# Best entries' rows and conditioning sums behind the linear attention's last step, in a fused decoder block on one Trainium2 core

## The chip, the cores and the metric

The kernel runs on one core of a Trainium2 chip. A core has a matrix engine (TensorE, PE in the profile), a vector engine (VectorE, DVE), an activation engine (ScalarE, ACT), a general engine (GpSimd, POOL) and a queue engine that issues transfers (SyncE, SP). Each engine runs its instructions in the order in which they were written to it and waits at an instruction whose inputs or buffers aren't ready. The metric is the device time of one execution in microseconds (us).

## The reference

One layer of a decoder block for 1024 tokens of width 1024. Two branches work on the same normalized input: a gated linear attention in chunks of 64 tokens, and a chunked gated MLP. Their gated outputs are added, projected by `w_out`, and added to the input. Then an expert mixer with product keys adds, for each token and each of 8 heads, the 16 best of 16384 rank-one experts. The norm ahead of each part has a scale and a shift that a dense layer (`w_ada`) makes from the conditioning vector `c`.

```
q, k, v, g, al, sgu, sgv, gate_a, gate_s = split(modulate(rms_norm(x), shift, scale) @ w_in)
state = diag(a_t) state + k_t^T v_t;  o_t = q_t state          # 4 heads, dk 128, dv 256
x = x + gate * ((norm(o) * silu(g), gated MLP) @ w_out)
h2 = modulate(rms_norm(x), shift2, scale2)
s = keys(h2 @ w_q);  entries, weights = top-16 of (top-16 x top-16)
x = x + gate2 * sum over heads and entries: weight * gelu(h2 . down[e]) * up[e]
```

(`modulate(h, shift, scale)` is h (1 + scale) + shift.)

## The kernel before, in words

The tokens are worked on in two halves of 512, each four blocks of 128. For a half, the columns of the input projection are streamed in groups of 512: V0, V1, QK0, the attention's heads 0 and 1, QK1, heads 2 and 3, and then the gates and the MLP; after them come `w_out` and `w_q`. A group is eight steps (`stream`, L1262), one for each 128 rows of its weights. In a step a weight tile `wt` arrives through SP's queue (L1248), ScalarE rounds it to `wh` (L1251), DVE takes the rest `wl = wt - wh` (L1252), and TensorE runs three products for each of four accumulators (L181 to L189). There are four `wt`, four `wh` and `wl`, and four accumulator banks.

After every step `step()` gives turns to queues of side work, which are Python generators that issue a few instructions and yield. Those that matter here:

- The **conditioning sums** (`ada_row`, L1139, with `ada_acc`, L1099): rows of `w_ada`, 128x1024 at a time (`wada`, L1103, on SP's queue, like the stream's weights), are multiplied by a column of `c` and added up on DVE, the first by L1106 and the other seven by L1108. This is done in the first half. The finished rows are joined by L1150 and L1154.
- The **routing** of the half before: `rare` (L391 to L447) handles the few tokens whose entries need another look; it gathers their scores from DRAM (L428, on POOL) and takes their maxima (L204 and on).
- The **direct rows** (`direct_rows`, L739): the best entry of every token and head of the first half, 4 blocks x 8 heads = 32 "entries", worked on during the second half. For each, POOL gathers a row of the down table and a row of the up table for each of 128 tokens (L752); DVE takes the dot product with `h2` (L764), ScalarE the GELU (L766), DVE the weight (L767, one column), and DVE adds the weighted up-row to the block's sum (L773; the first head of a block goes to L769 or a multiply).

The wide rows (`wada`, `adacc`, `uvd`, and the attention's outputs `ot`, which hold four) share one pool of eight 128x1024 tiles.

The attention's head (`gla_head`, L1402) transposes the keys (L1406), makes the in-chunk products (L1411, L1412), masks them by one DVE instruction, the *copy* into `at` (L1414), and goes through four token blocks: a state product (L1420), the output from `at` and from the state (L1422, L1423), and the *state update* on DVE (L1424). Ahead of it the queries leave their accumulators through L1378 to L1380 and the keys through L1395 to L1398. Side work gets its turns here too: `qdir.pump(RD)` (L1417), four times a head.

A pump has a rate: at 0.62 it advances its queue 62 times in 100 calls. `RD` is that rate for the direct rows in the stream's steps and in the heads. What a program order gives is then only a proposal: a scheduler goes over the instructions of all engines with its own model of their durations and fixes the order on each engine. `tc.issue_after(ins)` adds to an instruction the rule that it stands behind `ins` on its engine; `hlast`, `zlast` are earlier uses of it.

## Time and profile before

| | us |
|---|---|
| median of 3 runs | 1461.24 (1458.94 to 1463.65) |
| profiled execution, whole | 1465.81 |
| its span, first to last instruction | 1464.1 |
| TensorE busy | 1360.1 |
| VectorE busy | 1093.3 |
| ScalarE busy | 736.0 |
| GpSimd busy | 292.2 |
| mean granted TensorE clock | 0.967 |

A row such as `L764 DVE ... uvd<-uvd,h2d` is an instruction or a group of them: line of the kernel, engine, operation, and the tiles written and read. Brackets hold the idle time of the engine just ahead and what ended it. TensorE's matmuls take less time at a higher granted clock; a clock of 0.5 means half of full speed.

### The profile page before, as it was taken

The numbers are of one execution on the slowest core, as the hardware profiler recorded it, in microseconds if no ns is written. First come the engines' busy times: TensorE is split into PE (matmuls) and PEld (weight loads), VectorE is DVE, ScalarE is ACT, GpSimd is POOL, SyncE is SP. The second block draws the span as 40 slices with busy tenths as digits, with TensorE's granted clock in tenths as the row PEclk, the third lists the DMA queues.
The fourth block names the chain that finished last, engine by engine and source line by source line (L and its number), as shares of the span: only waits on it lengthen the run. The fifth ranks groups of instructions, "written<-read, shape, count | busy, mean of one in ns | idle before, by whom it ended". The sixth has DMA issues, their size and how long they took to land.

```text
span 1464.1 us, 19632 instructions
## 1 busy us (share of the span) xinstructions
PE 1360.1 (93%) x6004; PEld 1041.2 (71%) x6004; DVE 1093.3 (75%) x3114; ACT 736.0 (50%) x1611; POOL 292.2 (20%) x275
## 2 busy tenths in 40 slices
PE   3999999999998999998989999999988999888996
PEld 2778867888876887776777777887767876444553
DVE  6684768433467688988779888778889877888775
ACT  4464333333345545474434677566655555555542
POOL 0000001000000022432352133221111123543331
PEclk7999999999998999998999999999998999999998
DMA  9652544323349554767587689896687678998984
GB/s 323 218 188 96 195 150 147 108 94 102 131 152 318 175 202 147 257 203 255 195 293 261 220 308 348 294 351 217 225 330 260 213 246 315 345 357 312 404 305 167
DMA packets 120836, 345.00 MB, mean 236 GB/s; under 512 B 15033, under 2 KB 24505, under 8 KB 108690
## 3 DMA queue, kind: packets, MB, share of 16 engines
q0 software_dynamic: 32064, 165.95, 31.2%
q1 hardware_dynamic: 70992, 133.20, 27.2%
q10 hardware_dynamic: 17666, 44.53, 8.5%
q8 instruction: 48, 0.79, 0.2%
q14 instruction: 66, 0.54, 0.1%
HBM read 319.40 MB, written 24.23 MB: 235 GB/s over the span
## 4 chain that ended last, share of the span: by engine, by line
PE 58%; DMA 13%; DVE 12%; issue 9%; ACT 4%; POOL 2%; ACTq 0%; SPq 0%; DVEq 0%; POOLq 0%
PE mm L181 10%; PE mm L182 10%; PE mm L184 10%; PE acc L606 6%; PE mm L187 4%; PE mm L188 4%; PE mm L189 4%; DMA wada<-in_w_ada_dram 3%; DMA uvd<-in_down_dram,dix 2%; DMA uv<-in_tab_dram,ix 2%; DVE wl L1252 2%; POOL uvd L752 1%; DVE uv L580 1%; PE aux L1645 1%; PE hps L578 1%
## 5 line engine op out<-in xcount | busy, mean ns | idle before, releaser
L1251 ACT ACTIVATE wh<-wt 128x512 fp32r<-128x512 f32 x368 | 228.4, 628 | 311.1 <-PE mm L182 123.5
L1252 DVE TENSOR_TENSOR wl<-wt,wh 128x512 fp32r<-128x512 f32 x368 | 248.3, 685 | 145.6 <-ACT wh L1251 73.4
L181 PE MATMUL mm<-wh,hTh 128*128 128x512 f32 x672 | 266.1, 398 | 2.4 <-ACT wh L1251 2.3
L182 PE MATMUL mm<-wh,hTl 128*128 128x512 f32 x672 | 262.9, 393 | 0.0
L184 PE MATMUL mm<-wl,hTh 128*128 128x512 f32 x672 | 211.1, 396 | 0.0
L181 PEld LDWEIGHTS mm<-wh,hTh 128*128 128x128 f32 x672 | 127.2, 189 | 35.9 <-ACT wh L1251 5.9
L182 PEld LDWEIGHTS mm<-wh,hTl 128*128 128x128 f32 x672 | 127.0, 189 | 26.2
L184 PEld LDWEIGHTS mm<-wl,hTh 128*128 128x128 f32 x672 | 125.6, 189 | 27.8 <-issue 1.5
L525 POOL DMA_INDIRECT uv<-in_tab_dram,ix x74 | 79.7, 1077 | 250.3 <-ACT ix L557 176.0
L187 PE MATMUL mm<-wh,hTh 128*128 128x512 f32 x224 | 91.7, 418 | 10.1 <-ACT hTh L1209 5.5
L182 PE MATMUL mm<-hTl,wh 128*128 128x512 f32 x240 | 96.0, 400 | 0.0
L181 PE MATMUL mm<-hTh,wh 128*128 128x512 f32 x240 | 95.4, 397 | 0.0
L188 PE MATMUL mm<-wl,hTh 128*128 128x512 f32 x224 | 90.0, 402 | 0.8 <-DVE wl L1252 0.8
L189 PE MATMUL mm<-wh,hTl 128*128 128x512 f32 x224 | 88.3, 396 | 0.0
L580 DVE SCALAR_TENSOR_TENSOR uv<-uv,hps 128x512 f32<-128x512 f32 x112 | 75.0, 681 | 17.7 <-DMA uv<-in_tab_dram,ix 9.8
L187 PE MATMUL mm<-hTh,wh 128*128 128x256 f32 (+1 forms) x208 | 71.9, 350 | 7.6 <-DVE q L1379 6.8
L188 PE MATMUL mm<-hTl,wh 128*128 128x256 f32 (+1 forms) x208 | 70.9, 342 | 3.2 <-DVE hTl L173 3.2
L184 PE MATMUL mm<-hTh,wl 128*128 128x512 f32 x240 | 70.7, 396 | 0.3 <-DVE wl L1252 0.3
L752 POOL DMA_INDIRECT uvd<-in_down_dram,dix x32 | 36.9, 1154 | 168.0 <-DVE ts L359 44.7
L189 PE MATMUL mm<-hTh,wl 128*128 128x256 f32 (+1 forms) x208 | 69.7, 340 | 0.7 <-DVE wl L1252 0.7
L618 DVE SCALAR_TENSOR_TENSOR vl<-uv,r,vh 128x512 fp32r<-128x512 f32 x84 | 61.6, 746 | 10.0 <-ACT vh L617 7.3
L606 PE MATMUL acc<-uv,W 128*128 128x512 f32 x128 | 62.7, 613 | 5.6 <-ACT W L595 4.3
(933 smaller groups left out, 2896.2 us busy)
## 6 DMA issues: line engine op xcount, KB each, us to landing
wt<-in_w_inp_dram SPq DMA_DIRECT2D x224, 256.0 KB
wt<-in_w_qp_dram SPq DMA_DIRECT2D x80, 256.0 KB
wada<-in_w_ada_dram SPq DMA_DIRECT2D x32, 512.0 KB
wt<-in_w_outp_dram SPq DMA_DIRECT2D x64, 256.0 KB
wada<-in_w_ada_dram SPq DMA_DIRECT2D x32, 256.0 KB
s_d<-so ACTq DMA_DIRECT2D x28, 256.0 KB
xr<-in_x_dram ACTq DMA_DIRECT2D x8, 512.0 KB
x_d<-x ACTq DMA_DIRECT2D x8, 512.0 KB
```

What stands on the lines that cost most here:

```text
L181: nc.tensor.matmul(ps, lh, rh, start=False, stop=False)
L182: nc.tensor.matmul(ps, *((lh, rl) if feat else (ll, rh)), start=False, stop=False)
L184: nc.tensor.matmul(ps, *((ll, rh) if feat else (lh, rl)), start=False, stop=False)
L187: nc.tensor.matmul(ps, lh, rh, start=first, stop=False)
L188: nc.tensor.matmul(ps, lh, rl, start=False, stop=False)
L189: return nc.tensor.matmul(ps, ll, rh, start=False, stop=last).ins
L525: nc.gpsimd.indirect_dma_start(out=dst[:], out_offset=None, in_=src, in_offset=off)
L580: nc.vector.scalar_tensor_tensor(uv[0][:, sl], uv[0][:, sl], 1.0, hps, op0=OP.mult, op1=OP.mult, accum_out=r[:, 2 + n:3 + n])
L606: ins = nc.tensor.matmul(acc[:, sl], W, v[:, sl], start=first, stop=last).ins
L618: nc.vector.scalar_tensor_tensor(vl, v, r[:, 5:6], vh.bitcast(F32), op0=OP.mult, op1=OP.subtract)
L1251: nc.scalar.activation(wh, wt, AF.Identity)
L1252: nc.vector.tensor_tensor(wl, wt, wh.bitcast(F32), op=OP.subtract)
```

## The change

Four edits. (1) A list `crit` holds the last issued DVE instruction of the attention's chain: the last query or key operation (L1380, L1398), the copy (L1414) or a state update (L1424). The dot products and adds of the direct rows and the conditioning sums from the second on are issued behind it on DVE (`behind_crit`). (2) The direct rows' rate in the heads is 0.75 in place of 0.62, and in the stream's steps it is 1 in the first five of a group's eight steps and 0 in the last three. (3) `ada_acc` issues the load of the weights' row of step k+1 ahead of its sum of step k, with a yield between. (4) `rare` yields three times in place of once after the gather of its scores.

```diff
--- before.py
+++ after.py
@@ -45,7 +45,7 @@
 EB = 2
 WS = 4
 WT = 4
-RD = 0.62
+RD = 0.75
 UVC = 4
 RING = (1, 0, 1, 0, 2, 0)
 RING9 = (2, 0, 1, 2, 0, 2, 1, 0, 2)
@@ -428,7 +428,8 @@
         nc.gpsimd.indirect_dma_start(out=sc.rearrange("p c k -> p (c k)"), out_offset=None,
                                      in_=s_g[gi].rearrange("b p (h k) -> (b p h) k", h=PH),
                                      in_offset=bass.IndirectOffsetOnAxis(ap=ix, axis=0))
-        yield
+        for _ in range(3):
+            yield
         tv = r2.tile([P, 1, 2, TOPK], F32, name="qtv")
         ti = r2.tile([P, 1, 2, TOPK], U32, name="qti")
         for c in range(2):
@@ -734,7 +735,10 @@
         while b not in done:
             qr.pump()
 
-    zlast = []
+    zlast, crit = [], []
+
+    def behind_crit():
+        return tc.issue_after(crit[0]) if crit else nullcontext()
 
     def direct_rows(t4, bs):
         todo = [(b, h) for b in bs for h in range(PH)]
@@ -761,7 +765,8 @@
                 y = rowp.tile([P, D], F32, name="yd", tag="row")
             u, v = ents.pop(k)
             r = r2.tile([P, 2], F32, name="rdr", bufs=4)
-            nc.vector.scalar_tensor_tensor(u, u, 1.0, h2s[b], op0=OP.mult, op1=OP.mult, accum_out=r[:, 0:1])
+            with behind_crit():
+                nc.vector.scalar_tensor_tensor(u, u, 1.0, h2s[b], op0=OP.mult, op1=OP.mult, accum_out=r[:, 0:1])
             with tc.issue_after(zlast[0]):
                 nc.scalar.activation(r[:, 1:2], r[:, 0:1], AF.Gelu)
             nc.vector.tensor_tensor(r[:, 1:2], r[:, 1:2], dcol(dgtq, b, h), op=OP.mult)
@@ -770,7 +775,8 @@
             elif h == 0:
                 nc.vector.tensor_scalar(y, v, r[:, 1:2], None, op0=OP.mult)
             else:
-                nc.vector.scalar_tensor_tensor(y, v, r[:, 1:2], y, op0=OP.mult, op1=OP.add)
+                with behind_crit():
+                    nc.vector.scalar_tensor_tensor(y, v, r[:, 1:2], y, op0=OP.mult, op1=OP.add)
             if h == PH - 1:
                 nc.scalar.dma_start(y_d[b], y)
                 summed.add(b)
@@ -1098,15 +1104,25 @@
 
         def ada_acc(c):
             acc = t4("adacc")
-            for k in range(KD):
+            wts = []
+
+            def fetch(k):
                 wt = t4("wada")
                 nc.sync.dma_start(wt, w_ada[k * P:(k + 1) * P, c * D:(c + 1) * D])
+                wts.append(wt)
+
+            fetch(0)
+            for k in range(KD):
+                if k + 1 < KD:
+                    fetch(k + 1)
+                yield acc
+                wt = wts.pop(0)
                 if k == 0:
                     with tc.issue_after(hlast[1]):
                         nc.vector.tensor_scalar(acc, wt, sc[:, 0:1], None, op0=OP.mult)
                 else:
-                    nc.vector.scalar_tensor_tensor(acc, wt, sc[:, k:k + 1], acc, op0=OP.mult, op1=OP.add)
-                yield acc
+                    with behind_crit():
+                        nc.vector.scalar_tensor_tensor(acc, wt, sc[:, k:k + 1], acc, op0=OP.mult, op1=OP.add)
 
         def ada_cols(kp):
             accs = []
@@ -1267,6 +1283,7 @@
                     weights_ahead(len(srcs) if pre else LOOK + 1)
                     ws = [made.pop(0) for _ in srcs]
                     body(k, ws, pss)
+                    rate["d"] = 1.0 if k < 5 else 0.0
                     step()
                 for i in range(npsum):
                     evac(i, pss[i])
@@ -1377,7 +1394,7 @@
                         q4 = v4c(qs)
                         nc.vector.scalar_tensor_tensor(q4[:, :, 0], p4[:, :, 0], DK ** -0.5, e4[:, :, 0], op0=OP.mult, op1=OP.mult)
                         nc.vector.scalar_tensor_tensor(q1, p4[:, :, 1], DK ** -0.5, e4[:, :, 1], op0=OP.mult, op1=OP.mult)
-                        nc.vector.tensor_tensor(q4[:, :, 1], q1, last(0), op=OP.mult)
+                        crit[:] = [nc.vector.tensor_tensor(q4[:, :, 1], q1, last(0), op=OP.mult).ins]
                         qk[h] = [qs, q1]
                     else:
                         kk = gl.tile([P, 4, 3, 64], F32, name="kk")
@@ -1395,7 +1412,7 @@
                         nc.vector.tensor_tensor(kk[:, :, 0:3:2], p4, v4c(eGi), op=OP.mult)
                         nc.vector.tensor_tensor(kk[:, :, 1], p4[:, :, 0], d4[:, :, 0], op=OP.mult)
                         nc.vector.tensor_tensor(k4[:, :, 1], p4[:, :, 1], d4[:, :, 1], op=OP.mult)
-                        nc.vector.tensor_tensor(k4[:, :, 0], kk[:, :, 1], last(1), op=OP.mult)
+                        crit[:] = [nc.vector.tensor_tensor(k4[:, :, 0], kk[:, :, 1], last(1), op=OP.mult).ins]
                         qk[h] += [kk, kt]
                 return f
 
@@ -1411,7 +1428,7 @@
                     nc.tensor.matmul(aps_[:, p, 0:64], kk[:, p, 0:2], qs[:, p * P:p * P + 64], start=True, stop=True)
                     nc.tensor.matmul(aps_[:, p, 64:P], kk[:, p, 1:3], q1[:, p], start=True, stop=True)
                 a = at[h % 2]
-                nc.vector.copy_predicated(a, amask.unsqueeze(1).to_broadcast([P, 4, P]), aps_)
+                crit[:] = [nc.vector.copy_predicated(a, amask.unsqueeze(1).to_broadcast([P, 4, P]), aps_).ins]
                 hc = slice(h * DV, (h + 1) * DV)
                 for p in range(4):
                     qdir.pump(RD)
@@ -1421,7 +1438,8 @@
                     ops = gauxt([P, DV])
                     nc.tensor.matmul(ops, a[:, p], vt[p][:, hc], start=True, stop=False)
                     nc.tensor.matmul(ops, qs[:, p * P:(p + 1) * P], s_in, start=False, stop=True)
-                    nc.vector.scalar_tensor_tensor(s_out, s_in, eglt[h][:, p, 2:3], sps, op0=OP.mult, op1=OP.add)
+                    crit[:] = [nc.vector.scalar_tensor_tensor(s_out, s_in, eglt[h][:, p, 2:3], sps,
+                                                              op0=OP.mult, op1=OP.add).ins]
                     nc.scalar.activation(ot[p][:, hc], ops, AF.Identity)
                     jk = gl.tile([P, DV], F32, name="jk", bufs=1)
                     nc.scalar.activation(jk, ot[p][:, hc], AF.Square, accum_out=sso[:, p, h:h + 1])
```

The scheduler turns these into the following orders. The lines of the changed file are a few higher: L769 is what was L764 (dot), L772 was L767, L779 was L773 (add), L1122 was L1106 and L1125 was L1108 (conditioning sum), L1166 and L1170 were L1150 and L1154, L1268 was L1252 (`wl`), L1314 was L1297, L1431 was L1414 (copy), L1441 was L1424 (state update).

VectorE in the first half, from head 2's copy (into `at_309`) on, before:

```order
L1414 COPY_PREDICATED at_309<-amask,gaux 128x512
L1424 SCALAR_TENSOR_TENSOR S_1_304<-S_0_303,egl_894,aux 128x256
L1108 SCALAR_TENSOR_TENSOR adacc<-wada,sc,adacc 128x1024
L1252 TENSOR_TENSOR wl<-wt,wh 128x512 x2
L1108 SCALAR_TENSOR_TENSOR adacc<-wada,sc,adacc 128x1024
L1252 TENSOR_TENSOR wl<-wt,wh 128x512
L1108 SCALAR_TENSOR_TENSOR adacc<-wada,sc,adacc 128x1024
L1424 SCALAR_TENSOR_TENSOR S_0_303<-S_1_304,egl_894,aux 128x256
L1108 SCALAR_TENSOR_TENSOR adacc<-wada,sc,adacc 128x1024
```

and in the changed kernel:

```order
L1431 COPY_PREDICATED at_309<-amask,gaux 128x512
L1125 SCALAR_TENSOR_TENSOR adacc<-wada,sc,adacc 128x1024 x2
L1268 TENSOR_TENSOR wl<-wt,wh 128x512 x4
L1166 TENSOR_TENSOR adarow<-adarow,aux 1x512 x2
L1170 SCALAR_TENSOR_TENSOR adarow<-adarow,nrow 1x1024
L1268 TENSOR_TENSOR wl<-wt,wh 128x512
L1122 TENSOR_SCALAR adacc<-wada,sc 128x1024
L1441 SCALAR_TENSOR_TENSOR S_1_304<-S_0_303,egl_893,aux 128x256
L1441 SCALAR_TENSOR_TENSOR S_0_303<-S_1_304,egl_893,aux 128x256
```

Head 2's first state update (`S_1_304`) stood right behind the copy; now two conditioning sums, four `wl`, the joining of rows, another `wl` and the first product of the next sum stand between.

VectorE a little later, up to head 3's copy (into `at_311`) and its first state updates, before:

```order
L1108 SCALAR_TENSOR_TENSOR adacc<-wada,sc,adacc 128x1024 x2
L1424 SCALAR_TENSOR_TENSOR S_0_303<-S_1_304,egl_894,aux 128x256
L1108 SCALAR_TENSOR_TENSOR adacc<-wada,sc,adacc 128x1024
L1252 TENSOR_TENSOR wl<-wt,wh 128x512
L1106 TENSOR_SCALAR adacc<-wada,sc 128x1024
L1252 TENSOR_TENSOR wl<-wt,wh 128x512
L1108 SCALAR_TENSOR_TENSOR adacc<-wada,sc,adacc 128x1024
L1414 COPY_PREDICATED at_311<-amask,gaux 128x512
L1424 SCALAR_TENSOR_TENSOR S_1_307<-S_0_306,egl_899,aux 128x256
L1252 TENSOR_TENSOR wl<-wt,wh 128x512
L1424 SCALAR_TENSOR_TENSOR S_0_306<-S_1_307,egl_899,aux 128x256
```

and in the changed kernel:

```order
L1441 SCALAR_TENSOR_TENSOR S_1_304<-S_0_303,egl_893,aux 128x256
L1441 SCALAR_TENSOR_TENSOR S_0_303<-S_1_304,egl_893,aux 128x256
L1268 TENSOR_TENSOR wl<-wt,wh 128x512 x2
L1441 SCALAR_TENSOR_TENSOR S_1_304<-S_0_303,egl_893,aux 128x256
L1441 SCALAR_TENSOR_TENSOR S_0_303<-S_1_304,egl_893,aux 128x256
L1268 TENSOR_TENSOR wl<-wt,wh 128x512
L1431 COPY_PREDICATED at_311<-amask,gaux 128x512
L1441 SCALAR_TENSOR_TENSOR S_1_307<-S_0_306,egl_898,aux 128x256
L1441 SCALAR_TENSOR_TENSOR S_0_306<-S_1_307,egl_898,aux 128x256
L1314 BN_STATS bst<-svg 128x6 x2
L1441 SCALAR_TENSOR_TENSOR S_1_307<-S_0_306,egl_898,aux 128x256
```

The conditioning sums that stood among head 2's state updates and ahead of head 3's copy are gone from there; the next three stand behind head 3's updates.

VectorE in the second half, from head 2's last state update (`S_0_303`) to head 3's first two, before:

```order
L1424 SCALAR_TENSOR_TENSOR S_0_303<-S_1_304,egl_5839,aux 128x256
L1252 TENSOR_TENSOR wl<-wt,wh 128x512
L764 SCALAR_TENSOR_TENSOR uvd,rdr<-uvd,h2d 128x1024
L1252 TENSOR_TENSOR wl<-wt,wh 128x512
L767 TENSOR_TENSOR rdr<-rdr,dgt_0_140 128x1
L773 SCALAR_TENSOR_TENSOR yd<-uvd,rdr,yd 128x1024
L764 SCALAR_TENSOR_TENSOR uvd,rdr<-uvd,h2d 128x1024
L1414 COPY_PREDICATED at_311<-amask,gaux 128x512
L767 TENSOR_TENSOR rdr<-rdr,dgt_1_141 128x1
L1424 SCALAR_TENSOR_TENSOR S_1_307<-S_0_306,egl_5844,aux 128x256
```

and in the changed kernel:

```order
L1441 SCALAR_TENSOR_TENSOR S_0_303<-S_1_304,egl_5828,aux 128x256
L769 SCALAR_TENSOR_TENSOR uvd,rdr<-uvd,h2d 128x1024
L1268 TENSOR_TENSOR wl<-wt,wh 128x512
L772 TENSOR_TENSOR rdr<-rdr,dgt_0_140 128x1
L769 SCALAR_TENSOR_TENSOR uvd,rdr<-uvd,h2d 128x1024
L772 TENSOR_TENSOR rdr<-rdr,dgt_0_140 128x1
L1431 COPY_PREDICATED at_311<-amask,gaux 128x512
L779 SCALAR_TENSOR_TENSOR yd<-uvd,rdr,yd 128x1024
L1441 SCALAR_TENSOR_TENSOR S_1_307<-S_0_306,egl_5833,aux 128x256
```

The add that stood ahead of head 3's copy stands behind it now, ahead of head 3's first state update, and the copy follows on a dot whose entry is one earlier: 26 dots and 21 adds come before the copy in place of 27 and 22. Further ahead, two dots and an add that stood before head 0's state updates stand between them. From L204 of `rare` in the second half to the query evictions (L1378 before) the rows of both orders are the same, and so is the place of L428 in GpSimd's order. The loads of `wada` on SP's queue are spread among more loads of `wt`.

## The prediction

> **What bounds the kernel now.** I read the first parts of the page, then TensorE's waits, then the timeline at the three longest waits in the stretch that the change touches, then the granted clock around them.
>
> ```profile
> span 1464.1 us, 19632 instructions
> PE 1360.1 (93%) x6004; PEld 1041.2 (71%) x6004; DVE 1093.3 (75%) x3114; ACT 736.0 (50%) x1611; POOL 292.2 (20%) x275
> PE 58%; DMA 13%; DVE 12%; issue 9%; ACT 4%; POOL 2%; ACTq 0%; SPq 0%; DVEq 0%; POOLq 0%
> ```
>
> TensorE is busy for 1360.1 of 1464.1 us, so at most 104 us are idle in all, and a change of order on VectorE (DVE) can win only what TensorE waits for plus what its clock loses after a wait. The chain gives DVE 12% and DMA 13%. TensorE's waits say which instructions those are (columns: total us, times, longest):
>
> ```profile
> PE mm L187 <- DVE q L1379: 6.8, 1, 6.8
> PE gaux L1422 <- DVE rdr L767: 4.2, 1, 4.2
> PE gaux L1422 <- DVE at L1414: 3.4, 1, 3.4
> ```
>
> Call the 3.4 wait A (first half), the 6.8 wait B and the 4.2 wait C (both second half). A in the timeline (start, duration, engine, line; in brackets the idle time before and what ended it):
>
> ```profile
> 187.60 0.75 DVE L1106 TENSOR_SCALAR adacc<-wada,sc 128x1024 f32<-128x1024 f32 x1 [2.22 <-DMA wada<-in_w_ada_dram]
> 190.26 0.39 PE L188 MATMUL mm<-wl,hTh 128*128 128x512 f32 x1
> 190.49 0.40 PE L189 MATMUL mm<-wh,hTl 128*128 128x512 f32 x1
> 192.32 1.28 DVE L1108 SCALAR_TENSOR_TENSOR adacc<-wada,sc,adacc 128x1024 f32<-128x1024 f32 x1 [3.37 <-DMA wada<-in_w_ada_dram]
> 193.52 0.72 DVE L1414 COPY_PREDICATED at<-amask,gaux 128x512 f32<-128x512 int32 x1
> 194.29 0.70 PE L1422 MATMUL gaux<-vt,at 128*128 128x256 f32 x2 [3.40 <-DVE at L1414]
> ```
>
> Head 3's masked copy (L1414), which TensorE needs, stands behind a conditioning sum (L1108), and that sum waited 3.37 us for its weights' row. C is the same picture with a gathered row of the best entries:
>
> ```profile
> 748.87 1.28 DVE L773 SCALAR_TENSOR_TENSOR yd<-uvd,rdr,yd 128x1024 f32<-128x1024 f32 x1 [3.79 <-DMA uvd<-in_up_dram,dix]
> 750.21 1.23 DVE L764 SCALAR_TENSOR_TENSOR uvd<-uvd,h2d 128x1024 f32<-128x1024 f32 x1
> 751.36 0.72 DVE L1414 COPY_PREDICATED at<-amask,gaux 128x512 f32<-128x512 int32 x1
> 752.14 1.22 PE L1422 MATMUL gaux<-vt,at 128*128 128x256 f32 x2 [4.17 <-DVE rdr L767]
> ```
>
> The page names L767 there; it is an operation on one column behind the copy, and the copy at 751.36 is what was missing. B is different:
>
> ```profile
> 662.02 0.49 DVE L204 MAX8 qtv<-qsc 128x8 f32<-128x128 f32 x2 [3.10 <-DMA qsc<-s_d,qix]
> 664.20 0.39 PE L189 MATMUL mm<-hTh,wl 128*128 128x512 f32 x1
> 670.51 0.42 DVE L1378 SCALAR_TENSOR_TENSOR qs<-mm,eG 128x256 f32<-128x256 f32 x1
> 671.40 0.77 PE L187 MATMUL mm<-hTh,wh 128*128 128x512 f32 x1 [6.82 <-DVE q L1379]
> ```
>
> DVE loses 3.10 us on the rare tokens' score gather and works off its backlog until 670.51; only then do the query evictions free TensorE's banks. What a wait costs beyond itself is in the windows (us, busy, granted clock, DMA share, GB/s):
>
> ```profile
> 186.00:190.90 4.90, 4.89 (x30) 1.00 0.46 134
> 194.30:199.00 4.70, 4.70 (x14) 0.64 0.54 167
> 664.60:671.40 6.80, 0.00 (x0) 0.65 0.96 360
> 671.40:676.70 5.30, 5.29 (x13) 0.50 0.73 259
> 752.10:756.00 3.90, 3.86 (x11) 0.57 0.93 337
> 800.00:1250.00 450.00, 428.58 (x1982) 0.98 0.77 276
> ```
>
> Behind A 4.70 us ran at 0.64, which loses 4.70 x 0.36 = 1.7; behind B 5.30 x 0.50 = 2.65; behind C 3.90 x 0.43 = 1.7. So A is worth 5.1, B 9.5, C 5.9, at most 20.5 us together.
>
> [...]
>
> **The change part by part.** The durations of what is moved:
>
> ```profile
> L764 DVE SCALAR_TENSOR_TENSOR uvd<-uvd,h2d x32: 1204/1218/1240, 519.2 to 773.2; 128x1024 f32<-128x1024 f32 x32
> L773 DVE SCALAR_TENSOR_TENSOR yd<-uvd,rdr,yd x28: 1256/1278/1285, 526.2 to 785.8; 128x1024 f32<-128x1024 f32 x28
> L1108 DVE SCALAR_TENSOR_TENSOR adacc<-wada,sc,adacc x28: 1264/1284/1289, 68.5 to 226.6; 128x1024 f32<-128x1024 f32 x28
> L1150 DVE TENSOR_TENSOR adarow<-adarow,aux x8: 667/668/676, 101.7 to 240.9; 1x512 f32<-1x512 f32 x8
> ```
>
> No operation is added or removed: 32 dots, 28 adds and 28 conditioning sums run as before, and the DMAs are the same in number and size. All of the effect is order.
>
> *Wait A, conditioning sums behind the critical step, rows fetched one ahead.* In the new order head 3's copy stands behind one `wl` and head 2's state updates, and no conditioning sum stands between head 2's first state update and head 3's last one; the next three sums come after it. TensorE also has the eight split matmuls that it had between the products of L1411 and L1422 ahead of the transposes now, so the copy is asked for about 2 us earlier, measured from the end of L1411: a matmul every 0.23 us (190.26 to 190.49), eight of them 1.8 us. The copy itself takes 0.72, of which two `aux` matmul pairs cover some, so I leave 0.5 us of idle time. Gain: 3.40 - 0.5 + 1.7 = 4.6.
> The other side is head 2. Between its copy and its first state update now stand two sums (2 x 1.28), four `wl` (4 x 0.69), two row adds (2 x 0.67), one 1.21-us row operation, another `wl` and the first product of the next sum (0.75): 9.3 us. TensorE's second state product (L1423) was moved behind some 46 more matmuls, about 46 x 0.23 = 10.6 us, so it is covered if those sums don't wait. They can wait:
>
> ```profile
> DVE adacc L1108 <- DMA wada<-in_w_ada_dram: 13.7, 13, 3.4
> SPq L1103 <- DMA wada<-in_w_ada_dram: 24.3, 11, 3.4
> ```
>
> The wait is 1.05 us on average (13.7/13), and fetching a step ahead takes most of an average wait away; the longest, 3.4, would pass the cover of 1.3 by 2.1. Against the fetch stands SP's own queue: the rows' loads wait there for a free buffer (24.3 us in 11 waits, so 2.2 each), the stream's weights wait behind them, and each step ahead holds one buffer more out of the eight. I take -0.6 for head 2 and -0.5 for the weights; the bounds are 0 and -2.1 - 2.2 = -4.3. Net of A: +3.5, between +0.3 and +5.1.
>
> *Wait C, direct rows.* In the new order 26 dots and 21 adds stand ahead of head 3's copy, where 27 and 22 stood. What the copy waits for last is then the 26th dot, which began at 743.14 before, and not the 22nd add at 748.87. But the pace of these rows is set by gathers, as the first of these rows shows, and the gather of the next entry goes out when a dot or add has freed its buffer:
>
> ```profile
> DVE uvd L764 <- DMA uvd<-in_down_dram,dix: 16.0, 9, 5.2
> DVE yd L773 <- DMA uvd<-in_up_dram,dix: 4.9, 2, 3.8
> 719.15 1.22 DVE L764 SCALAR_TENSOR_TENSOR uvd<-uvd,h2d 128x1024 f32<-128x1024 f32 x1 [2.92 <-DMA uvd<-in_down_dram,dix]
> 743.14 1.23 DVE L764 SCALAR_TENSOR_TENSOR uvd<-uvd,h2d 128x1024 f32<-128x1024 f32 x1 [0.48 <-DMA uvd<-in_down_dram,dix]
> ```
>
> From 719.15 to 743.14 five entries pass, 4.8 us each. In the new order two dots and an add that stood ahead of head 0's state updates now stand between them, so the chain of gathers runs up to 0.75 of an entry late, 3.6 us: the 26th dot begins between 743.1 and 746.8, the copy between 744.4 and 748.0, and TensorE, which stopped at 748.0, waits 0 to 0.7 for it. The 22nd add now stands between the copy and head 3's first state update. With its gather at 748.87 to 752.5 it ends at 750.1 to 753.8, the update straight behind it, and TensorE can use about 1.7 us of other work meanwhile (to 749.7): a wait of 0.9 to 4.6 in place of 4.17. Best, 3.3 + 1.7 = +5.0; worst, -0.4 - 0 = -0.4, and with a further add behind it, -3.8 - 1.7 = -5.5. I take the middle of the first two, +2.5 with its share of the clock.
>
> *Rows in five of eight steps, 0.75 in the heads.* Before, 32 steps gave 32 x 0.62 = 19.8 entries and the heads' 16 pumps 9.9, 29.7 in all; the rest was drained after head 3. Now 4 x 5 = 20 and 16 x 0.75 = 12, exactly 32. The drain of two entries (2 x 2.5 us of DVE) goes away, and it was hidden: TensorE has no wait on L764 or L773 in its list. Worth 0. The two dots and the add among the state updates of head 0 are 2 x 1.22 + 1.28 = 3.7 us of DVE where TensorE has split matmuls to run; bounds 0 and -3.7, taken -1.0.
>
> *Three yields after the rare gather.* The place of that gather in POOL's order and of MAX8 (L204) in DVE's order, with all rows from there to L1378, are the same in both orders. So B stays: 0, and 9.5 if it went after all.
>
> *What follows.* Behind the heads the order of the later groups, of the routing and of the first entries is reshuffled on all engines. Between 800 and 1250 TensorE is idle for 450 - 428.6 = 21.4 us, in waits of which nearly all are short; a reshuffle can win or lose some fifth of that. Taken 0, with 4 to either side.
>
> **Sum.** +3.5 + 2.5 - 1.0 + 0 = 5.0 us. The profiled execution took 1465.81 (span 1464.1 and 1.7 around it), so it would take 1460.8; it lies 4.6 above the median of the runs, 1461.24, and on that scale the forecast is **1456.2 us**.
>
> **The rivals.** *Only A is won:* C's wait moves to the state update behind the 22nd add, whole. Then 3.5 - 1.0 - 0.4 = +2.1, so 1459. For it speaks the 3.79-us wait on that very gather; against it, that one entry less stands ahead of the copy.
> *B goes too:* the rare score chain is pulled away from the query evictions, 1456.2 - 9.5 = 1446.7. For it: three steps are worth 3 x 24 matmuls at some 0.23, far more than the 3.10 that the gather was late. Against it: the order there is unchanged.
> *Slower, gathers in front of state updates:* an add that waits for a gather now stands ahead of the first state update in heads 1 to 3, and each costs TensorE 3.79 and 1.7 of clock, 16.5 in all. With A's 4.6 and C's 5.9 won that is +6.0: 1467. It decides as soon as the gather chain lags by more than about one entry (4.8 us) in head 1; for it speaks that POOL's gathers run two at a time with the DMA at 0.93 to 0.96 busy; against it, that the adds waited for an up-row twice in the whole run, 4.9 us together, once over 3.
> *The order changes but not the waits:* DVE does the same work against the same arrivals, A's wait moves into head 2 and C's into S: 1461.
>
> **How the numbers follow.** A measurement of this kernel can tell about 0.3%, 4.4 us, from no change. Forecast 0.45 (own range 1451 to 1460: 0.35 faster, 0.10 same); only A 0.20 (0.03 / 0.15 / 0.02 faster, same, slower); B goes too 0.10 (faster); gathers in front 0.15 (0.03 same, 0.12 slower); no waits changed 0.10 (0.01 / 0.07 / 0.02). Sums: faster 0.49, same 0.35, slower 0.16. The bounds of the terms add up to 1461.2 - 5.1 - 5.0 - 4 = 1447 on the one side; on the other the slower rival gives 1467. The range, with the last tenth on either side left out: 1448 to 1466.
>
> **What would show it.** Right: TensorE's list has no wait of over 1 us on L1414's successor in the first half, and DVE's rows before head 3's copy there are a `wl` and state updates; the wait on the query eviction is still 6 to 7 us and has half clock behind it; at head 3 of the second half the wait is 1 to 4 us and names the state update. Wrong: a wait for `wada` in head 2 ahead of the first state update; a wait of over 3 us in heads 0 to 2 of the second half behind L773's successor; B under 3 us; or more than 25 us of idle TensorE between 800 and 1250.

## The result, and the profile after

The changed kernel is slower: 1477.09 us median (1470.40 to 1479.62) against 1461.28 for the kernel before, a ratio of 1.0111, 95% interval 1.0075 to 1.0148. The forecast was 1456.2, faster by 5; the range, 1448 to 1466, doesn't hold it.

The profiled execution was the shortest of the four, 1470.40 us, and the one of the kernel before (1465.81) lay 4.6 above its median, so the two profiles show a smaller difference than the medians. The page of the changed kernel, the first lines:

```profile
span 1468.7 us, 19651 instructions
PE 1356.1 (92%) x6004; PEld 1043.5 (71%) x6004; DVE 1091.8 (74%) x3114; ACT 727.7 (50%) x1607; POOL 304.4 (21%) x275
```

TensorE worked 4.0 us less than before (1360.1) and the span is 4.6 us longer, so 8.6 us more of it are idle. TensorE's waits of the changed kernel name where (L1396 was L1379, L1431 was L1414, L1501 was L1483):

```profile
PE mm L187 <- DVE q L1396: 8.3, 2, 6.6
PE mm L187 <- ACT sg L1501: 6.4, 1, 6.4
PE gaux L1439 <- DVE at L1431: 2.9, 1, 2.9
```

The 3.4-us wait A is gone, B is there (6.6), C went from 4.17 to 2.9, and a wait of 6.4 has come up on an eviction by ScalarE (ACT), at 873 us, 110 us behind the last head. Before, the longest wait on this line was 1.5:

```profile
PE mm L187 <- ACT sg L1483: 2.9, 2, 1.5
```

The windows of the changed kernel (us, busy, granted clock, DMA share, GB/s):

```profile
188.00:194.00 6.00, 6.00 (x32) 1.00 0.12 42
199.00:210.00 11.00, 8.35 (x37) 1.00 0.55 191
747.70:750.60 2.90, 0.01 (x1) 1.00 0.50 202
750.60:754.40 3.80, 3.80 (x11) 0.55 0.90 288
800.00:1250.00 450.00, 421.38 (x1941) 0.96 0.75 271
```

**Where A went.** Around head 3 TensorE runs without a gap at full clock (188 to 194), as forecast. Then 2.65 us are lost between 199 and 210. DVE and TensorE there:

```profile
188.94 0.73 DVE L1431 COPY_PREDICATED at<-amask,gaux 128x512 f32<-128x512 int32 x1 [1.99 <-PE gaux L1429]
204.24 1.28 DVE L1125 SCALAR_TENSOR_TENSOR adacc<-wada,sc,adacc 128x1024 f32<-128x1024 f32 x1 [0.99 <-DMA wada<-in_w_ada_dram]
205.44 3.65 DVE L1483 SCALAR_TENSOR_TENSOR ot<-ot,rso,glw 128x256 f32<-128x256 f32 x9
209.01 0.69 DVE L1268 TENSOR_TENSOR wl<-wt,wh 128x512 fp32r<-128x512 f32 x1
209.75 1.21 PE L184 MATMUL mm<-wl,hTh 128*128 128x512 f32 x4 [2.65 <-DVE wl L1268]
```

The conditioning sums that no longer stand in the heads stand right behind them: five between 197 and 205.5, two of which still wait for their weights' row (0.57 and 0.99), then nine products of 3.65 us together, and the `wl` that TensorE needs stands behind all of them. Over the whole stretch the two kernels, before and then after, give the same busy time:

```profile
130.00:300.00 170.00, 166.58 (x741) 0.99 0.44 143
```
```profile
130.00:300.00 170.00, 166.38 (x747) 1.00 0.42 143
```

3.4 us idle before, 3.6 after; only the clock is a hundredth better, 1.7 us. In a second profile of the changed kernel (f1 below) the wait at the same `wl` is 2.92 us and half clock follows it (0.83 on average from 210 to 220, where the first profile has 1.00), so that this gain is gone too. The wait has moved in every profile: the ten of kernels with the sums' edit show 2.65 to 3.31 us at this `wl`, between 209 and 215, and none at head 3's copy; the ten without it show 1.8 to 3.4 us at the copy, between 191 and 198.

**Where C went.** The copy now waits for the dot ahead of it, and that dot for its gather:

```profile
748.20 1.23 DVE L769 SCALAR_TENSOR_TENSOR uvd<-uvd,h2d 128x1024 f32<-128x1024 f32 x1 [6.09 <-DMA uvd<-in_down_dram,dix]
749.82 0.71 DVE L1431 COPY_PREDICATED at<-amask,gaux 128x512 f32<-128x512 int32 x1
750.59 1.11 PE L1439 MATMUL gaux<-vt,at 128*128 128x256 f32 x2 [2.89 <-DVE at L1431]
751.62 0.47 DVE L1441 SCALAR_TENSOR_TENSOR S<-S,egl,aux 128x256 f32<-128x256 f32 x1
```

The dot that began at 743.14 before begins at 748.20. The state update behind the add cost TensorE nothing here; in the second profile, where the copy was waited for 2.11 us, the update cost another 1.30.

**Where the time comes from.** Between 800 and 1250 us TensorE is idle for 450 - 421.4 = 28.6 us, 21.4 before, and its clock is 0.96 there, 0.98 before. The largest single piece:

```profile
866.19 0.39 PE L189 MATMUL mm<-wh,hTl 128*128 128x512 f32 x1
868.90 1.23 DVE L586 SCALAR_TENSOR_TENSOR uv<-uv,hr 128x1024 f32<-128x1024 f32 x1 [5.12 <-DMA uv<-in_tab_dram,ix]
870.16 0.20 ACT L589 ACTIVATE r<-r 128x1 f32<-128x1 f32 x1 [5.78 <-DVE uv L586]
872.36 0.60 ACT L1501 ACTIVATE sg<-mm 128x512 f32<-128x512 f32 x1
873.01 0.80 PE L187 MATMUL mm<-wh,hTh 128*128 128x512 f32 x1 [6.42 <-ACT sg L1501]
```

It is A and C once more, on another engine: a routed entry's dot waits 5.12 us for its gathered row, ScalarE's GELU for that dot, and the eviction that frees TensorE's accumulators is queued behind the GELU, with a table load of 1.28 us on ScalarE right ahead of it, at 871.06. TensorE then runs at half clock until 877 (0.50 from 873 to 877, 0.99 from 877 to 880). No edit of the change touches these instructions; the scheduler set them in this order.

The stream shows where the kernel falls behind. The 229th rounding of its weights to `wh` (L1251 before) starts at 767.3 us before, at the end of the heads; in the two profiles of the changed kernel it starts 1.4 and 0.1 us earlier. The 353rd starts at 1169.5 before, and 9.5 and 14.3 us later in the changed kernel. So the heads gave next to nothing, and between 767 and 1169 some 11 and 14 us are lost.

### The profile page after: what moved, and what is told of

It is laid out like the page before. It is cut to its first block, busy times and chain, and to the rows that moved or that the text cites. A ratio compares the mean times of both kernels' runs of the same rounds, so it can differ in the third digit from the quotient of the medians.

```text
span 1468.7 us, 19651 instructions
## 1 busy us (share of the span) xinstructions
PE 1356.1 (92%) x6004; PEld 1043.5 (71%) x6004; DVE 1091.8 (74%) x3114; ACT 727.7 (50%) x1607; POOL 304.4 (21%) x275
## 5 line engine op out<-in xcount | busy, mean ns | idle before, releaser
L1268 DVE TENSOR_TENSOR wl<-wt,wh 128x512 fp32r<-128x512 f32 x368 | 248.8, 685 | 141.5 <-PE mm L184 70.5
L526 POOL DMA_INDIRECT uv<-in_tab_dram,ix x74 | 83.1, 1123 | 258.5 <-ACT ix L558 170.8
L579 PE MATMUL hps<-hh,E 128*128 128x512 f32 x132 | 61.3, 466 | 6.4 <-ACT ts__6830 L552 2.6
```

Source lines behind the costliest of these rows:

```text
L526: nc.gpsimd.indirect_dma_start(out=dst[:], out_offset=None, in_=src, in_offset=off)
L579: nc.tensor.matmul(hps, Ej, hh[:, sl], start=True, stop=False)
L1268: nc.vector.tensor_tensor(wl, wt, wh.bitcast(F32), op=OP.subtract)
```

## The experiments

Times are ratios to the kernel before on the same chip, in per cent, with the 95% interval. The single executions of one kernel in one set spread over 5 to 19 us, so one profile can lie some us from its kernel's median. Two executions far above the others of their kernel are left out of the ratios: 4647.6 us of e4 and 1485.05 us of h1.

### Each edit by itself

The edits are those of the diff, one at a time:

```
e1_ada    + behind_crit() on adacc; fetch(k + 1) ahead of the sum of k
e2_dir    + behind_crit() on the direct rows' dots and adds
e3_rate   + RD = 0.75;  rate["d"] = 1.0 if k < 5 else 0.0
e4_rare   + for _ in range(3): yield
```

> Only the conditioning sums behind the critical step, with their weights' row one step ahead; direct rows, rates and the rare routing as before. Its VectorE order equals the changed kernel's up to the end of the first half's heads and the kernel before's from there to about 830 us, then it is an order of its own up to the routing of the second half. Late-order theory (the loss comes from the order of the work behind the heads, which any early edit reshuffles): 3 to 5 us ahead at 300 us, still so at 760, then 5 to 15 lost, end 1463 to 1474. Gathers-in-front theory (direct rows ahead of state updates lose): 1456 to 1458. Weights-crowding theory (fetching ahead delays the stream): behind already at 300 us, 1463 or more.

> Only the direct rows' dots and adds behind the critical step, at the old rates. Late-order theory: within 2 us of before at 760, end 1463 to 1474. Gathers-in-front theory: 4 to 10 us behind at 760 already, and the same at the end. Forecast's own mechanism alone (wait at head 3 shorter, nothing else): 1458 to 1459.

> Only the rates: 0.75 in the heads, 1 in five of eight steps and 0 in three. VectorE order as before to about 780 us. Late-order theory: equal to before at 760, end anywhere from 1459 to 1474. Gathers-in-front theory: no effect without the edges, 1459 to 1463.

> Only the three yields after the rare gather. VectorE's order is the same as before but for some 150 instructions around 1190 to 1290 us. All theories: within 3 us of before, 1458 to 1464; more than that would say that the place of the second half's rare work matters by itself.

Measured: sums +0.28 (0.00 to 0.57), direct rows +0.91 (0.63 to 1.19), rates -0.10 (-0.42 to 0.22), yields +0.11 (-0.13 to 0.35). The direct rows' edges carried most of the loss in this set, but not in the heads: their C is a little larger, B smaller, as their TensorE waits show, and their loss came later (at 767 us the stream is 4.7 us ahead of the kernel before, so that gathers in front of state updates aren't what costs the time): TensorE was idle for 28 us between 800 and 1250 (table below), where before it was 21.

```profile
PE gaux L1427 <- DVE at L1419: 4.9, 1, 4.9
PE mm L187 <- DVE q L1384: 4.6, 1, 4.6
```

The sums' and the rates' runs also have late orders of their own and lost little or nothing. So not every new order costs 10 us. The 3 to 5 us that the sums alone were expected to be ahead at 300 us aren't there either: the stream is 0.7 us ahead at that place, and 1.4 behind at 767. A few us can't be told in one profile anyway: at 300 us the nine other profiles without the sums' edit lie between 4.0 us ahead of the kernel before and 2.7 behind it.

### Which part of the change

```
f1_after_again     the changed kernel
f2_after_h_first   + with tc.issue_after(h2l gather): first uv gather of a routed entry
f3_adds_only       behind_crit() on the direct rows' adds alone
f4_all_but_direct  the change - behind_crit() on the direct rows
```

> The changed kernel once more, for a second profile and for times beside those of this call. All theories: 1470 to 1480, 0.6 to 1.2% above before. In the profile the first gather of the routed entries' rows stands ahead of the gather of the rare tokens' h rows on GpSimd, and the routed entries run 10 us or more behind the kernel before by 950 us.

> The changed kernel with one edge more: the first gather of a routed entry's rows is issued behind the gather of the rare tokens' h rows, as it stood in the kernel before; VectorE's order differs from the changed kernel's only in some 60 instructions around 780 to 830 us. Late-start theory (the swapped gathers let the routed entries start late, and they stay late to the end): entries at most 5 us behind at 950, end 1460 to 1466. Late-order theory (the whole order behind the heads is a worse one): no more than 3 us better than the changed kernel, 1470 to 1478.

> Only the direct rows' adds behind the critical step, not the dot products, at the old rates. GpSimd's gathers are swapped as in the changed kernel; VectorE's order behind the heads is one of its own. Late-start theory: as the dots alone, 1470 to 1477. Late-order theory: anywhere from 1460 to 1477. Gathers-in-front theory: the adds are what stands ahead of state updates, so 1470 or more and behind already at 760 us.

> The change without the edges on the direct rows: conditioning sums, one row ahead, rates and the three yields. GpSimd's gathers stand as before. VectorE's order is the changed kernel's behind about 1000 us, but for pieces. Late-start theory: 1462 to 1468 (sum of the single edits: 1461 + 4 - 1.5 + 1.5). Late-order theory: 1470 or more, since most of the late order is that of the changed kernel.

Measured: the change again +1.03 (0.65 to 1.41), with the h rows first +0.66 (0.37 to 0.95), adds only -0.50 (-0.81 to -0.18), all but direct +0.27 (0.00 to 0.54). The late start of the entries through swapped gathers is not the cause: the adds-only run has the swap, its entries run 9.2 us behind at 950 us, about as those of f1 do (8.7), and it is faster than before. f2 says little of it, since its edge didn't bring the entries forward (9.4 us behind at 950); its median is 3.7 us below that of f1. f4, expected at 1470 or more by the late-order theory, came out at 1467.55. One row of f1 is worth showing beside f2. The 6-us eviction wait stands in the second profile of the changed kernel as well; with the edge, which altered some 60 of DVE's instructions there, it is 3.4:

```profile
PE mm L187 <- ACT sg L1501: 6.1, 1, 6.1
```
```profile
PE mm L187 <- ACT sg L1503: 3.4, 1, 3.4
```

At that stage I suspected the dots: both slow orders had them behind the step, and the adds alone didn't hurt.

### The dots, or one draw of the order

```
g1_no_dot_edge     the change - behind_crit() on the dots
g2_adds_and_rates  f3_adds_only + e3_rate
g3_dir_rate_066    e2_dir + RD = 0.66
g4_dir_rate_070    e2_dir + RD = 0.70
```

> The whole change except that the direct rows' dot products aren't issued behind the critical step (their adds still are). Dot theory (the dots behind the step make the loss): 1455 to 1464. Order-by-chance theory (each late order has its own waits, whatever edit made it): this one is new, 1455 to 1478.

> Direct rows' adds behind the critical step and the new rates; dots, conditioning sums and the rare routing as before. Dot theory: the single edits add up, -7 and -1.5, so 1452 to 1460. Order-by-chance theory: 1455 to 1478, the adds-only gain need not come back.

> The direct rows' dots and adds behind the critical step, at a rate of 0.66 in place of 0.62, nothing else. Its order behind the heads has less than half of its instructions in common with the order of the run with the edges alone. Dot theory: 1470 or more again. Order-by-chance theory: 1455 to 1478, a draw of its own.

> As the run before, at a rate of 0.70: one draw more. Dot theory: 1470 or more. Order-by-chance theory: 1455 to 1478; if both this one and the one at 0.66 are 1470 or more, chance is unlikely.

Measured: no dot edge +0.44 (0.11 to 0.77), adds and rates +0.28 (-0.04 to 0.59), dots at 0.66 -0.14 (-0.47 to 0.18), dots at 0.70 -0.37 (-0.64 to -0.09). The dot theory falls on both sides: without the dots' edges the change is still slower, and with them the kernel is no slower once the rate is 0.66 or 0.70. Nor do edits seem to add up: the adds' gain (-0.50) is gone when the rates (-0.10) are put beside it (+0.28).

### The sums by themselves, and the edges at 0.70

```
h1_sums_and_direct  the change - its rates (e1 + e2 + e4)
h2_direct_again     e2_dir
h3_edges_070        h1 + RD = 0.70
```

> The change without its rates: conditioning sums behind the critical step with their row ahead, direct rows behind it at 0.62, three yields. On VectorE the order from the end of the first half's heads to about 1190 us is word for word that of the run with the direct rows' edges alone. Forecast's term for the sums: 3.5 us faster than that run. Moved-wait reading of the traces (the wait at head 3 goes and comes back behind the heads, at the wl that the sums pile up ahead of): within 2 us of that run.

> The direct rows' edges alone at 0.62 again, beside the run before on the same chip: 1470 to 1478, 0.7 to 1.1% above the kernel before.

> All edges of the change, the row ahead and the three yields, with a plain rate of 0.70 in place of 0.75 and five of eight steps. About 90% of its VectorE order is that of the run of the direct rows' edges at 0.70, which was 0.4% faster than before; the rest, between 830 and 1190 us, is a new draw. Order-by-chance theory: 1453 to 1468, so clear of the changed kernel. If the edits themselves are slow: 1470 or more.

Measured: +0.56 (0.34 to 0.78), +0.39 (0.14 to 0.65), and -0.86 (-1.10 to -0.62), 1453.04 us. With VectorE's order held from the heads to about 1190 us, the sums' edit, together with the three yields, comes out 0.17% slower (0.56 - 0.39), 2.5 us, a little more than the 2 us expected of a moved wait. The two intervals overlap, so a loss isn't shown; a gain of 3.5 us, which would have put h1 at 0.15, lies outside h1's interval. That the wait moved is shown by the traces above.

The second run was expected at 0.7 to 1.1% and missed: the same program that lay at +0.91 came out at +0.39 on another chip. A kernel's ratio can thus differ by half a per cent between two sets, and differences of that size between kernels of different sets can't be told. The changed kernel itself repeated well (1.11 and 1.03).

The third run has the edges, the row ahead and the yields of the change, and is 0.86% *faster* than before at a plain rate of 0.70. It differs from the changed kernel in two lines:

```
-RD = 0.75
+RD = 0.70
-                    rate["d"] = 1.0 if k < 5 else 0.0
```

### An early end of the direct rows

```
i1_change_six_of_eight  the change, k < 6 for k < 5
i2_change_heads_090     the change, RD = 0.90
i3_before_070           the kernel before, RD = 0.70
```

> The changed kernel with the direct rows' rate 1 in six of eight steps in place of five; all else as changed. 24 + 12 pumps for 32 entries, so the direct rows end before head 3, near 755 us. Early-end theory (routed entries start sooner when the direct rows end sooner): 1450 to 1460, over 0.8% below the changed kernel. Order-by-chance theory: 1450 to 1478.

> The changed kernel with 0.90 in the heads in place of 0.75: 20 + 14.4 pumps, direct rows end near 760 us. Early-end theory: 1450 to 1460. Order-by-chance theory: 1450 to 1478.

> The kernel before with the direct rows' rate 0.70 in place of 0.62, no edge, nothing else. 22.4 + 11.2 pumps, direct rows end near 760 us. Early-end theory: 0.3 to 0.9% below the kernel before, as the run with the edges at 0.70. Order-by-chance theory: anything from 1450 to 1475.

Measured: +0.24 (-0.07 to 0.54), +0.44 (0.17 to 0.70), and -1.15 (-1.55 to -0.74), 1451.98 us in 5 runs. The last is the fastest kernel of all, and it is the kernel before with one constant changed and no edge, row ahead or yield of the change. In i2 the direct rows ended at 781, not early, so it tells nothing of an early end; in i1 they ended at 764 and the kernel was still not faster than before.

The rows of the direct dots (the last time is the start of the last one) of the changed kernel, and then of h3:

```profile
L769 DVE SCALAR_TENSOR_TENSOR uvd<-uvd,h2d x32: 1205/1222/1239, 515.9 to 778.9; 128x1024 f32<-128x1024 f32 x32
```
```profile
L769 DVE SCALAR_TENSOR_TENSOR uvd<-uvd,h2d x32: 1201/1218/1227, 517.1 to 766.7; 128x1024 f32<-128x1024 f32 x32
```

i3 has 764.4 there, g4 759.4, i1 764.1, the kernel before 773.2. So all three kernels at a plain 0.70 end their direct rows 6 to 14 us earlier than before and are faster by 0.37 to 1.15%, but i1 ends them as early and isn't, and the adds-only run ends them at 780.9 and is faster. An early end helps, or goes with what helps; it doesn't decide.

A rate of 0.70 needn't be luck, however. Three pairs of kernels differ in nothing but a plain rate of 0.62 or 0.70, and in all three 0.70 is faster: the kernel before and i3 (0 and -1.15), the direct rows' edges (+0.91 or +0.39, and -0.37), and h1 and h3 (+0.56 and -0.86). That is 0.8 to 1.4% each time. No run separates a benefit of the rate itself from the luck of three orders. In the three profiles at 0.70 the wait on head 3's copy in the second half is gone or 1.3 us, where it is 2.1 to 7.9 in all other profiles; but only g4's stream is ahead of the kernel before at 767 us. Why 0.70 is faster stays open.

### What goes with the time in all of them

Three numbers of each profile: the last of the 84 additions of routed entries to the first half's sums (L625 before, start of the last), TensorE's idle time between 800 and 1250, and by how much the stream's stretch from its 229th to its 353rd rounding (767 to 1169 us before) takes longer than in the kernel before.

| kernel | ratio, % | last entry, us | idle 800-1250, us | stream 767-1169, us |
|---|---|---|---|---|
| i3, before at 0.70 | -1.15 | 1150 | 18 | -6 |
| h3, edges at 0.70 | -0.86 | 1152 | 17 | -7 |
| f3, adds only | -0.50 | 1161 | 22 | +2 |
| g4, direct at 0.70 | -0.37 | 1148 | 19 | -1 |
| g3, direct at 0.66 | -0.14 | 1150 | 21 | -8 |
| e3, rates | -0.10 | 1154 | 22 | -5 |
| before | 0 | 1155 | 21 | 0 |
| e4, yields | +0.11 | 1160 | 24 | +1 |
| i1, six of eight | +0.24 | 1164 | 28 | +10 |
| f4, all but direct | +0.27 | 1160 | 24 | +2 |
| e1, sums | +0.28 | 1161 | 18 | +1 |
| g2, adds and rates | +0.28 | 1170 | 28 | +13 |
| h2, direct | +0.39 | 1169 | 27 | +8 |
| g1, no dot edge | +0.44 | 1168 | 20 | 0 |
| i2, 0.90 in heads | +0.44 | 1176 | 27 | +10 |
| f2, h rows first | +0.66 | 1174 | 32 | +15 |
| e2, direct | +0.91 | 1166 | 28 | +8 |
| f1, the change | +1.03 | 1173 | 33 | +14 |
| the change | +1.11 | 1168 | 29 | +11 |

(h1's profile lay 12 us above its median and isn't used. That of i3 lay 11 us above its own, too; its row is the most doubtful of the table.) The rows behind the second column, for before, f1 and h3:

```profile
L625 PE MATMUL acc<-vh,e x84: 388/393/628, 801.1 to 1155.1; 128*128 128x512 f32 x84
```
```profile
L626 PE MATMUL acc<-vh,e x84: 388/393/775, 805.7 to 1172.5; 128*128 128x512 f32 x84
```
```profile
L626 PE MATMUL acc<-vh,e x84: 389/393/792, 801.0 to 1151.6; 128*128 128x512 f32 x84
```

The first entry of f1 starts 4.6 us later than in the kernel before, the last one 17.4. With the last entry at 1152 or earlier all four kernels are faster or not told from before; with it at 1166 or later all eight lie above it, by 0.28 to 1.11%, seven of them clearly (g2's interval takes in 0). But from this entry to the end it takes 299 to 311 us in every profile, so the last entry is for the most part a reading of how late the kernel already is. The idle time alone says less: e1 and g1 are slower with 18 and 20 us of it.

The stream's column says where kernels became late: eight lose 7 us or more between 767 and 1169, and these include all that are slower by 0.39% or more but g1, whose profile is 13 us behind at 767 already. In most kernels, then, the time is won or lost where the first half's routed entries, with their gathers, are threaded through the second half's streams, and the order there is what the edits change. That this relation holds is shown, with one profile for each kernel; that a late entry is what makes the end late, rather than both following from the same waits, is not.

## Why the prediction was wrong

**The failed step is "What follows".** The reshuffle behind the heads was put at 0 with 4 to either side. In the two profiles of the changed kernel the stream loses 10.9 and 14.5 us between 767 and 1169; TensorE's idle time between 800 and 1250 grew by 7.2 and 11.4 us, with a clock of 0.96 and 0.97 for 0.98. Of the 5.0 us that the heads were to give, 1.4 and 0.1 were there at 767. The number that would have shown it wrong, over 25 us idle there, was named and came out as 28.6. What failed was the size, and also the reasoning: "some fifth" of 21.4 us took the waits that were there as the stock that could vary, but a new order can put a gather wait ahead of an eviction, as the 6.4 us at 873 show. Why this order is a bad one, beyond such single waits, stays open.

**The range** was made unevenly. Its fast end adds up the bounds of the terms; its slow end is a rival's 1467. The terms' own slow bounds (A +0.3, C -0.4, head 0 -3.7, the reshuffle -4) give 1461.2 - 0.3 + 0.4 + 3.7 + 4 = 1469, and 1474 with the -5.5 of C.

**A (+3.5 net) was wrong in its sum.** The wait went, the clock held in the first profile (1.00 from 188 to 194 and from 199 to 220), and the cover in head 2 was right: the first state update there cost nothing. But the sums that were moved weren't priced where they land. Five of them and nine products stand ahead of a `wl`, and the wait came back there as 2.65 and 2.92. With the late order held no gain was measured: 2.5 us slower (not clear of 0) where 3.5 faster was forecast.

**C (+2.5) had the right cause, late gathers, and the wrong place.** The gathers lag by more than the 3.6 us allowed (5.1: 748.20 for 743.14), so the copy waited 2.89 and 2.11 and not 0 to 0.7, the first with half clock behind it (0.55 from 750.6 to 754.4). The wait at the state update, taken as 0.9 to 4.6, was 0 and 1.3. Of 4.17 some 1.3 and, the update counted, 0.8 are won; e1, e3, e4 and f4, without the edges there, waited 3.9 to 6.6 at this copy, so the 4.17 was itself one of many values. (The middle of the two bounds used, +5.0 and -0.4, is 2.3, not 2.5.)

**The direct rows' rates (0) were misread.** 20 + 12 = 32 pumps were counted as an end of the rows by head 3, one drain less. Their last dot moved from 773.2 to 778.9, and with the rates alone (e3) to 774.8: a pump's instructions can run later than the pump. The -1.0 for the direct rows in head 0 can't be told from 0: between 675 and 745 TensorE is idle 1.4 us longer than before, at a clock of 1.00 for 0.96.

**B (0) was right:** the yields left the order alone, and 6.55 us stood before the query evictions:

```profile
670.34 0.77 PE L187 MATMUL mm<-hTh,wh 128*128 128x512 f32 x1 [6.55 <-DVE q L1396]
```

Other edits shorten it: 4.4 us in h3, 4.1 in i3 and i1, 4.6 in e2.

**The rivals.** The slower one had the sign, but not the place: in both profiles of the change no wait on a state update came to more than 1.3 us. "The order changes but not the waits" describes the heads best, though A's wait moved behind head 3 and not into head 2, and C's stayed at the copy; it didn't see the loss either. "Only A is won" is wrong, since A wasn't. The chance of 0.16 for slower was too low: of the 17 changed kernels tried, four came out clearly faster than before, and eight slower, two of them just.

**The clock.** The sums for A and for the best case of C have the whole 1.7 us of clock come back while 0.5 and 0.9 us of waiting stay; that was my estimate. At A's copy no wait was left, and the clock is 1.00 from 188 to 194. At C's copy 2.89 us idle up to 750.59 were followed by half clock (0.55 from 750.6 to 754.4), as 4.17 before had been (0.57 from 752.1 to 756). In the profiles of the kernel before and of the changed kernel the granted clock is either whole or half; the half-speed stretches, 17 and 16 of them, but for the last of each, last 3.41 us or a whole multiple of that, up to 17.07, and within a profile they start on one grid of this step. (Clocks such as 0.55 above are means over a whole and a half part.) What a wait cost went, in most places, with how much of one window of the grid was idle. The window from 747.33 to 750.74 held 2.89 us of idle time, and half clock followed. The 2.65 us at 209 lie across a limit of the grid, 0.91 and 1.74 us in two windows, and cost no clock. In these two profiles, from the first record of the clock on (18.1 and 16.9 us), all 22 windows at whole clock with more than 2 us idle were followed by half clock, 9 of the 14 with 1.5 to 2 us, and two of the 527 with less.

## What to carry to other kernels

Where a scheduler sets the order, an edit's price is its own plus that of a new order of all work behind it: look how far the orders agree, and time two or three harmless neighbours of an edit before its sign is believed. Work that is moved out of the way of a critical step must be priced at the place where it lands, with all that is queued behind it there. And the constant beside an elaborate change may be worth more than the change: here a rate of 0.70 in place of 0.62, alone, gave 1.15% (five executions on one chip).

## What the runs showed of the hardware

Equal programs differ more from execution to execution than the three first times told: the kernel before lay between 1452.4 and 1476.3 us over its executions in the five sets of experiments, each on another chip, and by 16 to 19 us within each set; its medians lay between 1460.8 and 1467.0. One execution of e4 took 4647.6 us, at a granted clock of 1.00, for no reason that the record shows. A kernel's one profile is a draw too: the changed kernel was profiled at 1470.40 and at 1476.23 with the same order, and TensorE's idle time between 800 and 1250 was 4 us longer in the second. In the profiles of the kernel before and of the changed kernel TensorE's clock fell to half for 3.41 us or multiples of it, the last stretch of each aside, on one grid in each, and idle time of less than a whole window was followed by it: 2.89 us in the window from 747.33 were, 1.74 us in the window from 208.02 were not.
